# A two-layer attention encoder on one core: the feed-forward in 256x1024 weight tiles, half of them by Strassen's algorithm

## The chip, the core and the metric

The kernel runs on one core of one Trainium2 chip. The core has five engines that work side by side, each with its own queue that it takes strictly in order: TensorE (PE in the profile; its weight loads are shown apart as PEld), VectorE (DVE), ScalarE (ACT), GpSimd (POOL) and SyncE (SP), which here issues most DMAs. Engines wait for each other through semaphores. Matmuls read SBUF and add into PSUM, which has eight banks of 512 float32 columns for each of 128 partitions. The metric is the device time of one execution in microseconds, as a median of several runs; smaller is better. Shares, waits and durations come from a profile of one execution.

## The reference

256 tokens of width 2048 go through two layers, all in float32. Each layer is a norm and an attention, added to x, then a norm and a feed-forward, added to x. The change concerns the feed-forward alone:

```python
D_MODEL = 2048
SEQ = 256
D_FF = 4 * D_MODEL
...
def sq_relu_mlp(h, w1, w2):
    return jnp.square(jax.nn.relu(h @ w1)) @ w2
...
        g, w1, w2 = ffns[i]
        x = x + sq_relu_mlp(rms_norm(x, g), w1, w2)
    return rms_norm(x, final_norm)
```

So per layer there are 256 x 2048 by 2048 x 8192, then 256 x 8192 by 8192 x 2048. Layer 0 has 2-D neighbourhood attention with 16 heads, layer 1 a dilated attention with three groups of eight heads.

## The kernel before

**Two parts for each number.** TensorE multiplies in a format that is rounded against float32 (F32R). Every operand is therefore cut into a rounded part (`hi`, a cast on ScalarE) and the rest (`lo`, a subtraction on VectorE), which is what `split` does (L103 to L105: L104 the cast, L105 the subtraction). A product takes three matmuls: hi by hi, hi by lo, lo by hi.

**Steps.** The program is a list of 400 steps. Each takes one weight block [4 x 128, 512] of 1 MB. `load` fetches it with one DMA on SP's queue into one of three buffers (`wpool`); `prep` cuts one half of it, 1024 columns, into `wh` and `wl`, of which there are four buffers each (`hlpool`). The loop at the end of the program emits, for each step i, its four quarters on TensorE; the first half of step i + 2 is cut behind the second quarter, the other half behind the last, and the load of step i + 5 is issued there too. What else a step carries stands in its lists: `tasks` (a part on TensorE after a quarter, with a part that follows on other engines), `evac` (reads the finished sums), `post`. The order in every engine's queue is the order in which this loop writes it; no scheduler changes it.

**Feed-forward.** It runs over four groups g of 2048 hidden columns, in each of the two layers. A group is 16 steps for w1 and 16 for w2.

- w1 is `gemm_cols`: the weights stand still (each 128x128 piece is loaded into the array), and the activations `xT`, with the 256 tokens' hi and lo side by side, move. Per piece there is a matmul of 512 columns (L134) and one of 256 (L136), 16 such pairs a block. Sums come out with hidden columns on partitions, as the next product needs them. Behind every fourth block two sums each of 512 columns are taken out (a copy on ScalarE at L144, an addition on VectorE at L146), and `done` in `ffn` applies the norm's 1/rms and the squared ReLU (L471, L474) and cuts the result into `hT`.
- w2 is `gemm_rows`: the activations stand still, and the weights move, 24 matmuls of 512 columns a block (`products`, L155 to L157). Sums come out with tokens on partitions and are added to x (L271).

**Norms.** x is transposed on TensorE (L194) and multiplied by the gain, into two parts. 1/rms is applied behind the products. For w1 it is needed along the free axis, so `rows` (L229) spreads it with two small matmuls.

**PSUM.** Three pairs of banks collect sums (`ps_acc`); two single banks (`ps_misc`) serve transposes and attention.

Of the kernel before, what the change touches and what calls it, by code (L numbers as in the profile page):

```python
# [8 lines left out]
F32 = mybir.dt.float32  # L9
# [19 lines left out]
class Step:  # L29
    """One weight block [4 x 128, 512], the products that it takes part in (in four  # L30
    quarters) and the work that goes with them: tasks have a part on the tensor engine
    after a quarter, evac reads the finished sums, post follows."""

    def __init__(self, src, quarters):
        self.src = src
        self.quarters = quarters
        self.evac = []
        self.tasks = [[] for _ in range(4)]
        self.post = []


@with_exitstack
def tile_encoder(ctx: ExitStack, tc: tile.TileContext, ins, out):
    nc = tc.nc

    const = ctx.enter_context(tc.tile_pool(name="const", bufs=1))
    wpool = ctx.enter_context(tc.tile_pool(name="wpool", bufs=3))
    hlpool = ctx.enter_context(tc.tile_pool(name="hlpool", bufs=4))
    big = ctx.enter_context(tc.tile_pool(name="big", bufs=9))
    mid = ctx.enter_context(tc.tile_pool(name="mid", bufs=9))  # L50
    tmp = ctx.enter_context(tc.tile_pool(name="tmp", bufs=2))
    small = ctx.enter_context(tc.tile_pool(name="small", bufs=4))
    ps_acc = ctx.enter_context(tc.tile_pool(name="ps_acc", bufs=3, space=bass.MemoryType.PSUM))
    ps_misc = ctx.enter_context(tc.tile_pool(name="ps_misc", bufs=2, space=bass.MemoryType.PSUM))
# [11 lines left out]
    rope_c = const.tile([32, T], F32, name="rope_c")  # L66
    rope_s = const.tile([32, T], F32, name="rope_s")
# [4 lines left out]
    steps = []  # L72

    def load(i):
        if i >= len(steps):
            return
        s = steps[i]
        s.w = wpool.tile([P, 4, 512], F32, name="w", tag="w")
        s.hi, s.lo = [None] * 2, [None] * 2
        if i:  # L80
            nc.sync.dma_start(s.w, s.src)

    def load_half(i, u):
        nc.sync.dma_start(steps[i].w[:, 2 * u:2 * u + 2, :], steps[i].src[:, 2 * u:2 * u + 2, :])

    def prep(i, u):
        if i >= len(steps):
            return
        s = steps[i]
        hi = hlpool.tile([P, 2, 512], F32R, name="wh", tag="wh")  # L90
        lo = hlpool.tile([P, 2, 512], F32R, name="wl", tag="wl")
        part = s.w[:, 2 * u:2 * u + 2, :]
        if i:
            split(hi, lo, part)
        else:
            for a in range(2):
                split(hi[:, a], lo[:, a], part[:, a])
        s.hi[u], s.lo[u] = hi, lo
# [8 lines left out]
    def three(o, left, right, start, stop):  # L107
        """o += left.T @ right, both in two parts; the product of the two rests is below float32."""
# [5 lines left out]
    def gemm_cols(w, col, xT, nk, done):  # L114
        acc = {}
        made = []
        for k in range(nk):
            def quarter(s, n, k=k):
                if k == 0:
                    if s is steps[0]:  # L120
                        n = (0, 2, 1, 3)[n]
                    if n % 2 == 0:
                        acc[n // 2] = ps_acc.tile([P, 2, 512], F32, name="acc", tag="acc")
# [3 lines left out]
                for j in js:  # L127
                    o = acc[j // 2][:, j % 2, :]
                    cs = slice(j * P, (j + 1) * P)
                    for a in parts:  # L130
# [3 lines left out]
                        nc.tensor.matmul(o, s.hi[a // 2][:, a % 2, cs], xt.rearrange("p h t -> p (h t)"),  # L134
                                         start=first, stop=False)
                        nc.tensor.matmul(o[:, :T], s.lo[a // 2][:, a % 2, cs], xt[:, 0, :],  # L136
                                         start=False, stop=last)
            s = Step(block(w, k, col), quarter)
            steps.append(s)
            made.append(s)  # L140
        for j in range(2):
            def ev(j=j):
                b = tmp.tile([P, 2, T], F32, name="b", tag="b", bufs=2)
                nc.scalar.copy(b, acc[j][:, :, T:])  # L144
                z = tmp.tile([P, 2, T], F32, name="z", tag="z", bufs=2)
# [6 lines left out]
    def products(o, s, xt, a, ts_, start, stop):  # L152
        xh, xl = xt[:, a, 0, ts_], xt[:, a, 1, ts_]
        wh, wl = s.hi[a // 2][:, a % 2, :], s.lo[a // 2][:, a % 2, :]
        nc.tensor.matmul(o, xh, wh, start=start, stop=False)  # L155
        nc.tensor.matmul(o, xh, wl, start=False, stop=False)  # L156
# [674 lines left out]
```

## Time and profile before

| | us |
|---|---|
| median of 3 runs | 2322.12 (2321.59 to 2323.97) |
| span of the profiled execution | 2320.3 |
| busy: PE | 2300.7 |
| busy: DVE | 1406.0 |
| busy: ACT | 1092.6 |
| busy: POOL | 0.7 |
| all PE rows of w1 and of attention, L134 and L136 | 1178.5 and 935.0, x3328 each |
| all PE rows of w2, L155, L156, L157 | 399.5, 399.0, 398.9, x1024 each |

Of the feed-forward, L134 and L136 hold 128 of their 208 blocks. The lengths of matmuls overlap in the trace, since the next begins before the last has drained, so a matmul's price is the distance of starts and not the mean length. The idle time ahead of an engine's instruction is listed with what ended it; on an engine that is not the bound, it costs nothing by itself.

### The profile page before, as it was taken

The numbers are of one execution on the slowest core, as the hardware profiler recorded it, in microseconds if no ns is written. First come the engines' busy times: TensorE is split into PE (matmuls) and PEld (weight loads), VectorE is DVE, ScalarE is ACT, GpSimd is POOL, SyncE is SP. The second block draws the span as 40 slices with busy tenths as digits, with TensorE's granted clock in tenths as the row PEclk, the third lists the DMA queues.
The fourth block names the chain that finished last, engine by engine and source line by source line (L and its number), as shares of the span: only waits on it lengthen the run. The fifth ranks groups of instructions, "written<-read, shape, count | busy, mean of one in ns | idle before, by whom it ended". The sixth has DMA issues, their size and how long they took to land.

```text
span 2320.3 us, 29178 instructions
## 1 busy us (share of the span) xinstructions
PE 2300.7 (99%) x11956; PEld 1963.1 (85%) x11956; DVE 1406.0 (61%) x1635; ACT 1092.6 (47%) x1390; POOL 0.7 (0%) x6
## 2 busy tenths in 40 slices
PE   8999999999999999999999999999999999999998
PEld 7888888888888888888888888888888888888886
DVE  6666765654555555566777667756654654555654
ACT  6444545543443453455444544445543543543443
POOL 0000000000000000000000000000000000000000
PEclk9999999999999999999999999999999999999999
DMA  7555655555555555555555545454555555555553
GB/s 248 169 175 176 191 182 170 182 197 200 182 187 194 185 196 189 193 181 188 189 179 184 177 164 181 164 181 169 191 192 193 182 200 187 189 187 200 200 192 135
DMA packets 73862, 430.36 MB, mean 185 GB/s; under 512 B 19776, under 2 KB 20352, under 8 KB 22528
## 3 DMA queue, kind: packets, MB, share of 16 engines
q1 hardware_dynamic: 73056, 426.80, 54.3%
q8 instruction: 93, 1.52, 0.3%
q10 hardware_dynamic: 672, 1.70, 0.2%
q14 instruction: 41, 0.34, 0.0%
HBM read 426.38 MB, written 2.10 MB: 185 GB/s over the span
## 4 chain that ended last, share of the span: by engine, by line
PE 98%; DMA 1%; DVE 1%; ACT 0%; issue 0%; SPq 0%; ACTq 0%; DVEq 0%
PE acc L134 33%; PE acc L136 17%; PE acc L156 15%; PE acc L155 15%; PE acc L157 15%; PE misc L194 1%; DMA bias<-in_rpb_dram 0%; PE misc L111 0%; PE misc L110 0%; PE misc L109 0%; DVE wl L105 0%; PE misc L593 0%; PE misc L553 0%; PE misc L380 0%; ACT wh L104 0%
## 5 line engine op out<-in xcount | busy, mean ns | idle before, releaser
L105 DVE TENSOR_TENSOR wl<-w,wh 128x1024 fp32r<-128x1024 f32 (+1 forms) x802 | 972.8, 1221 | 735.8 <-ACT wh L104 733.6
L104 ACT CAST wh<-w 128x1024 fp32r<-128x1024 f32 (+1 forms) x802 | 834.9, 1049 | 936.9 <-PE acc L157 460.2
L134 PE MATMUL acc<-xT,wh 128*128 128x512 f32 x3328 | 1178.5, 399 | 0.9 <-ACT wh L104 0.9
L136 PE MATMUL acc<-xT,wl 128*128 128x256 f32 x3328 | 935.0, 281 | 2.3 <-DVE wl L105 2.3
L134 PEld LDWEIGHTS acc<-xT,wh 128*128 128x128 f32 x3328 | 626.4, 188 | 150.4 <-ACT wh L104 1.9
L136 PEld LDWEIGHTS acc<-xT,wl 128*128 128x128 f32 x3328 | 629.8, 189 | 3.7 <-DVE wl L105 3.2
L155 PE MATMUL acc<-wh,hT 128*128 128x512 f32 x1024 | 399.5, 390 | 0.0
L156 PE MATMUL acc<-wl,hT 128*128 128x512 f32 x1024 | 399.0, 390 | 0.0
L157 PE MATMUL acc<-wh,hT 128*128 128x512 f32 x1024 | 398.9, 390 | 0.0
L157 PEld LDWEIGHTS acc<-wh,hT 128*128 128x128 f32 x1024 | 192.3, 188 | 39.9
L155 PEld LDWEIGHTS acc<-wh,hT 128*128 128x128 f32 x1024 | 192.3, 188 | 39.7
L156 PEld LDWEIGHTS acc<-wl,hT 128*128 128x128 f32 x1024 | 192.3, 188 | 39.4
L155 PE MATMUL acc<-wh,xT 128*128 128x512 f32 x320 | 126.7, 396 | 0.0
L156 PE MATMUL acc<-wl,xT 128*128 128x512 f32 x320 | 125.2, 391 | 1.1 <-DVE wl L105 1.1
L157 PE MATMUL acc<-wh,xT 128*128 128x512 f32 x320 | 124.9, 390 | 0.0
L144 ACT COPY b<-acc 128x512 f32<-128x512 f32 x104 | 60.7, 586 | 64.8 <-PE acc L136 59.1
L146 DVE TENSOR_TENSOR z<-acc,b 128x512 f32<-128x512 f32 x104 | 71.5, 691 | 25.8 <-ACT b L144 25.2
L155 PE MATMUL acc<-wh,oT 128*128 128x512 f32 x192 | 76.6, 399 | 0.0
L157 PE MATMUL acc<-wh,oT 128*128 128x512 f32 x192 | 75.0, 391 | 0.0
L156 PE MATMUL acc<-wl,oT 128*128 128x512 f32 x192 | 74.9, 390 | 0.0
L156 PEld LDWEIGHTS acc<-wl,xT 128*128 128x128 f32 x320 | 60.2, 188 | 13.1 <-DVE wl L105 1.8
L157 PEld LDWEIGHTS acc<-wh,xT 128*128 128x128 f32 x320 | 60.1, 188 | 12.5
(123 smaller groups left out, 1044.9 us busy)
## 6 DMA issues: line engine op xcount, KB each, us to landing
w<-in_ffn_w_dram SPq DMA_DIRECT2D x256, 1024.0 KB, 4.8
w<-in_dil_wqkv_dram SPq DMA_DIRECT2D x72, 1024.0 KB, 4.8
w<-in_na_wqkv_dram SPq DMA_DIRECT2D x47, 1024.0 KB, 4.9
w<-in_na_wo_dram SPq DMA_DIRECT2D x16, 1024.0 KB, 4.9
w<-in_dil_wo_dram SPq DMA_DIRECT2D x8, 1024.0 KB, 4.8
bias<-in_rpb_dram SPq DMA_DIRECT2D x32, 96.0 KB, 8.7
out_dram<-x SPq DMA_DIRECT2D x8, 256.0 KB, 2.5
x<-in_x_dram SPq DMA_DIRECT2D x3, 512.0 KB, 7.8
```

Of the source, the lines that this page charges most:

```text
L104: nc.scalar.copy(dst_hi, src)
L105: nc.vector.tensor_tensor(out=dst_lo, in0=src, in1=dst_hi.bitcast(F32), op=ALU.subtract)
L134: nc.tensor.matmul(o, s.hi[a // 2][:, a % 2, cs], xt.rearrange("p h t -> p (h t)"), start=first, stop=False)
L136: nc.tensor.matmul(o[:, :T], s.lo[a // 2][:, a % 2, cs], xt[:, 0, :], start=False, stop=last)
L144: nc.scalar.copy(b, acc[j][:, :, T:])
L146: nc.vector.tensor_tensor(out=z, in0=acc[j][:, :, :T], in1=b, op=ALU.add)
L155: nc.tensor.matmul(o, xh, wh, start=start, stop=False)
L156: nc.tensor.matmul(o, xh, wl, start=False, stop=False)
L157: nc.tensor.matmul(o, xl, wh, start=False, stop=stop)
L194: nc.tensor.transpose(self.tp[:, a, tb * P:(tb + 1) * P], x[:, tb, kt * P:(kt + 1) * P], ident)
```

## The change

**Tiles and forms.** The feed-forward's w1 and w2 both go through a new `gemm_pair`, with activations standing still and tokens on partitions. A step's 1 MB is now a tile of 256 rows by 1024 columns of the weights, loaded by two DMAs of 512 KB. Eight steps make a pair of column blocks (`cp`): four "x" steps, then four "s" steps.

```diff
+    FF_ORDER = [("x", k) for k in range(4)] + [("s", k) for k in range(4, 8)]
+    FF_PAIRS = [k for kind, k in FF_ORDER if kind == "x"]
```

An "s" step is the plain product of 2 x 2 blocks (tokens halves by k halves, k halves by column blocks): 8 products of 3 matmuls, all of 512 columns. An "x" step does the same by Strassen's algorithm in Winograd's form, 7 products of 3 matmuls. It needs sums of weight blocks and of activation blocks. In `X`, each entry is bank, left operand, index of the right:

```diff
+        X = (("1", "A11", 2), ("2", "A12", 3), ("6", "S2", 6), ("7", "S3", 4), ("5", "S1", 5), ("4", "A22", 0),
+             ("3", "S4", 1))
...
+                def quarter(s, m, pair=pair, n=n):
+                    for bank, a, b in X[2 * m:2 * m + 2]:
+                        product(bank, left(pair, a), (s.hi[b], s.lo[b]), n == first_x[-1] and
+                                (bank in "1567" or not first_s))
```

**Cutting the weights.** `prep` now has four parts per step, behind the quarters of the step two ahead of it. An x step makes four sums on VectorE, their rounded parts on ScalarE (`hs`, 1536 columns at once), and rests on VectorE (`ls`) and GpSimd. `sums` has one buffer, `hs` and `ls` have two each. In an s step, GpSimd makes the rests of both halves in even steps and of one half in odd ones; VectorE makes the other:

```diff
+        if n == 0:
+            t = s.sums = part.pool.tile([P, 4, 512], F32, name="sums", tag="sums", bufs=1)
+            add(nc.vector, t[:, 0:2, :], w[:, 1:3, :], w[:, 0, :].unsqueeze(1).to_broadcast([P, 2, 512]))
+            add(nc.vector, t[:, 2, :], t[:, 1, :], w[:, 1, :])
+            add(nc.vector, t[:, 3, :], t[:, 2, :], w[:, 3, :])
+        elif n == 1:
+            hi, lo = two_parts(s, 1)
+            nc.scalar.copy(hi, w[:, 2:4, :])
+            subtract(nc.gpsimd, lo, w[:, 2:4, :], hi.bitcast(F32))
+            s.hs = part.pool.tile([P, 3, 512], F32R, name="hs", tag="hs", bufs=2)
+            nc.scalar.copy(s.hs, s.sums[:, 0:3, :])
+        elif n == 2:
+            ls = part.pool.tile([P, 3, 512], F32R, name="ls", tag="ls", bufs=2)
+            subtract(nc.vector, ls, s.sums[:, 0:3, :], s.hs.bitcast(F32))
...
+            elif s.kind == "s" and (u or s.even):
+                nc.scalar.copy(hi, part)
+                subtract(nc.gpsimd, lo, part, hi.bitcast(F32))
```

**Ends of a pair.** The sums of the x steps (banks 1, 5, 6, 7) are brought together into a tile `C` in SBUF while step s0 runs (`begin`: one copy on ScalarE, four operations on VectorE), and those of all steps (banks 2, 3, 4, S) are added while s3 runs (`end`: four operations on VectorE). A w2 pair then adds C to x with two operations of 1024 columns (`rows`).

**Hidden activations.** Behind a w1 pair, `squared_relu` takes eight operations on ScalarE during the next pair's x0. Then C must be transposed: four groups of four transposes stand in x2 and x3 of the next pair, behind their first and third quarter, all into one PSUM bank. Of the first w1 pair of a group the transposed values are copied out by ScalarE, and `sums_and_parts` makes the sums of activation blocks that the x steps of w2 need; of the second they are only cut in two:

```diff
+                    def post(r=r, held=held):
+                        c, half, pair = 2 * cp + r // 2, r % 2, 4 * cp + r
...
+                        if pair in FF_PAIRS:
+                            raw = scratch([P, 2, T], "h")
+                            nc.scalar.copy(raw, held["t"])
+                            sums[pair] = part.pool.tile([P, 2, 3, P], F32R, name="hs", tag="hsum", bufs=len(FF_PAIRS))
+                            sums_and_parts(raw, hT[c], half, sums[pair], nc.gpsimd)
+                        else:
+                            to = hT[c][:, 2 * half:2 * half + 2]
+                            split(to[:, :, 0, :], to[:, :, 1, :], held["t"])
+
+                    at(i + 2 + r // 2, pe, post, quarter=r % 2 * 2)
...
+        c = scratch([P, 3, P], "c")
+        a11, a21, a12, a22 = raw[:, 0, :P], raw[:, 0, P:], raw[:, 1, :P], raw[:, 1, P:]
+        subtract(nc.vector, c[:, 0, :], a11, a21)
+        subtract(nc.vector, a21, a21, a22)
+        subtract(nc.vector, c[:, 1, :], a11, a21)
+        subtract(nc.vector, c[:, 2, :], a12, c[:, 1, :])
+        hi, lo = (t[:, 2 * half:2 * half + 2, h, :] for h in range(2))
+        nc.scalar.copy(hi, raw)
+        nc.scalar.copy(sums[:, 0], c)
+        subtract(engine, lo, raw, hi.bitcast(F32))
+        subtract(engine, sums[:, 1], c, sums[:, 0].bitcast(F32))
```

**Memory.** PSUM is one tile of eight banks, given out by hand. SBUF has, beside the common tiles, one pool for the attention's tiles and one for the feed-forward's, in the same place, one at a time. 1/rms now applies to partitions, so `rows` (L229) is gone for the norms ahead of the feed-forwards. The attention's arithmetic stays.

**What moves in the queues.** First VectorE's queue where a group's w1 blocks run, before the change. `wl` is a rest of 1024 columns, `z` a sum of 512 that is taken out, `hT` a hidden part; the square brackets name whom an instruction waits for.

```order
L105 TENSOR_TENSOR wl<-w,wh 128x1024 [waits DMAHW7_49,PE_49,Activation_49]
L146 TENSOR_TENSOR z<-acc,b 128x512 [waits Activation_49] x2
L105 TENSOR_TENSOR wl<-w,wh 128x1024 [waits Activation_49]
L471 SCALAR_TENSOR_TENSOR z<-z,rbc 128x512 [waits DVE_49] x2
L105 TENSOR_TENSOR hT<-z,hT 128x2x256 [waits Activation_49] x2
L105 TENSOR_TENSOR wl<-w,wh 128x1024 [waits DMAHW0_49,PE_49,Activation_49]
```

And after the change, VectorE's queue from the rest of a w2 pair's last s step (L192) through the first two x steps of the next pair:

```order
L192 TENSOR_TENSOR wl<-w,wh 128x1024 [waits DMAHW6_49,Activation_49]
L130 TENSOR_TENSOR sums<-w 128x1024 [waits DMAHW1_49,DMAHW0_49]
L130 TENSOR_TENSOR sums<-sums,w 128x512 [waits DVE_49] x2
L127 TENSOR_TENSOR ls<-sums,hs 128x1536 [waits Activation_49]
L127 TENSOR_TENSOR wl<-sums,wh 128x512 [waits PE_49,Activation_49,Pool_49]
L130 TENSOR_TENSOR C<-C,banks 128x512 [waits PE_49]
L130 TENSOR_TENSOR sums<-w 128x1024 [waits DMAHW3_49,DMAHW2_49,DVE_49]
L130 TENSOR_TENSOR sums<-sums,w 128x512 [waits DVE_49] x2
L127 TENSOR_TENSOR C<-banks,C 128x512 [waits PE_49]
L130 TENSOR_TENSOR C<-C,banks 128x512 [waits PE_49]
L127 TENSOR_TENSOR ls<-sums,hs 128x1536 [waits Activation_49]
L130 TENSOR_TENSOR C<-C,banks 128x512 [waits PE_49]
```

Where VectorE had one rest of 1024 per half step, it now has sums, the rest `ls` behind ScalarE's cast of 1536, and the pair's end between them. Right behind these rows come two sums `x<-x,C` of 1024 columns.

Next TensorE's queue before the change, where the last w1 block of a group ends and its first w2 block begins:

```order
L134 MATMUL acc<-xT,wh 128x512
L136 MATMUL acc<-xT,wl 128x256
L134 MATMUL acc<-xT,wh 128x512
L136 MATMUL acc<-xT,wl 128x256
L155 MATMUL acc<-wh,hT 128x512 [waits Activation_49]
L156 MATMUL acc<-wl,hT 128x512 [waits DVE_49]
L157 MATMUL acc<-wh,hT 128x512
```

After the change, TensorE's queue at the third quarter of x2 and the first of x3, in a pair that follows the first w1 pair of a group (`xs` are the sums of activation blocks, `ident<-C` rows the transposes of hidden columns):

```order
L693 MATMUL banks<-ident,C 128x128 [waits Activation_49]
L693 MATMUL banks<-ident,C 128x128 x3
L196 MATMUL banks<-wh,xs 128x512
L197 MATMUL banks<-wl,xs 128x512 [waits Pool_49]
L198 MATMUL banks<-wh,xs 128x512
L196 MATMUL banks<-wh,xT 128x512
L197 MATMUL banks<-wl,xT 128x512 [waits Pool_49]
L198 MATMUL banks<-wh,xT 128x512
```

Before, w2's products followed w1's with nothing between them, and only a block's first products waited, for ScalarE and VectorE. Now the transposes stand between the products, their first one waits for ScalarE, and products of the lower parts wait for GpSimd.

Last ScalarE's queue in the same pair, from the last casts for x3 on. L702 is the copy of a group of transposes, L457 and L458 the rounded parts of hidden values and of their sums, L156 the cast for an s step:

```order
L174 CAST hs<-sums 128x1536 [waits DVE_49,PE_49]
L182 CAST wh<-w 128x512 [waits DMAHW6_49,PE_49,Pool_49]
L183 CAST wh<-sums 128x512 [waits DVE_49]
L702 COPY h<-banks 128x512 [waits PE_49]
L457 CAST hT<-h 128x2x256 [waits DVE_49,Activation_49]
L458 CAST hs<-c 128x384 [waits DVE_49]
L156 CAST wh<-w 128x1024 [waits DMAHW1_49,Pool_49]
L702 COPY h<-banks 128x512 [waits PE_49,Pool_49]
```

The copy that frees the transposes' bank stands behind the cast of VectorE's last sum for x3, and the next copy behind two casts that wait for VectorE and one for an s step. Before the change, ScalarE's queue in w1 blocks held the casts L104, the copies L144 and the squares L474 only.

More of the change, by code (lines that the diff above doesn't have):

```diff
@@ L482, in tile_encoder, with both @@
+            def both(q, tb):
+                return q["C"][:, 2 * tb:2 * tb + 2, :].rearrange("p a n -> p (a n)")
+            for cp in range(2):
+                gemm_pair(w2g, cp, hT, sums, FF_ORDER, lambda made, q, cp=cp: residual(made, q, cp),
+                          split_end=last and next_norm() in fin and cp == 1)
     ffn(norms[1], ins["ffn0_w1"], ins["ffn0_w2"], lambda: norms[2], begin_norm(2, True))
+    parts[len(steps)] = "attention"
     n2 = norms[2]
@@ L703, in tile_encoder @@
             steps[i].tasks[q].append((pe, post))
+    for i, n, f in later_after:
+        steps[i].after[n].append(f)
     def load_x(begin, end):
```

423 lines of the change are left out of this document (297 added, 126 removed).

## The prediction, made before the run

> **What bounds the kernel now.** I read the page first, then the waits, then the stretches of the feed-forward.
>
> ```profile
> span 2320.3 us, 29178 instructions
> PE 2300.7 (99%) x11956; PEld 1963.1 (85%) x11956; DVE 1406.0 (61%) x1635; ACT 1092.6 (47%) x1390; POOL 0.7 (0%) x6
> PEclk9999999999999999999999999999999999999999
> PE 98%; DMA 1%; DVE 1%; ACT 0%; issue 0%; SPq 0%; ACTq 0%; DVEq 0%
> ```
>
> TensorE is busy for 99% of the span at the full granted clock, and 98% of the chain that ended last is its own work. The waits of TensorE that the trace puts down to the engines that cut the weights are tiny, while VectorE spends its idle time waiting for the cast on ScalarE, and ScalarE for TensorE to give a buffer back:
>
> ```profile
> PE acc L136 <- DVE wl L105: 2.3, 3, 0.8
> PE acc L156 <- DVE wl L105: 1.1, 2, 0.6
> DVE wl L105 <- ACT wh L104: 733.6, 606, 3.3
> ACT wh L104 <- PE acc L157: 460.2, 292, 2.2
> ```
>
> So the time before is the number of matmuls times their spacing. What one group g of a feed-forward takes is seen in the stretches of one w1 half and one w2 half (length, then the busy time of PE, PEld, DVE, ACT, POOL, then clock, DMA share and GB/s):
>
> ```profile
> 407.00:495.60 88.60, 88.60 (x516) 77.64 (x515) 53.74 (x65) 47.17 (x60) 0.00 (x0) 1.00 0.54 185
> 495.60:583.00 87.40, 87.40 (x390) 72.48 (x389) 46.76 (x45) 36.86 (x38) 0.00 (x0) 1.00 0.57 193
> ```
>
> That is 88.6 + 87.4, about 176 us, and eight such groups make up some 1406 of the 2320 us. VectorE has about 100 us of work in 176, GpSimd none. The attention layers keep their arithmetic, and I count no change there.
>
> **What TensorE saves.** The spacings are read from starts far apart in steady stretches, since a matmul's own length overlaps the next:
>
> ```profile
> 451.79 0.40 PE L134 MATMUL acc<-xT,wh 128*128 128x512 f32 x1
> 461.49 0.40 PE L134 MATMUL acc<-xT,wh 128*128 128x512 f32 x1
> 699.67 0.39 PE L157 MATMUL acc<-wh,hT 128*128 128x512 f32 x1
> 732.99 0.39 PE L157 MATMUL acc<-wh,hT 128*128 128x512 f32 x1
> 1054.00 0.39 PE L157 MATMUL acc<-wh,hT 128*128 128x512 f32 x1
> 1054.23 0.60 PE L194 MATMUL misc<-ident,x 128*128 128x128 f32 x4
> 1054.59 0.47 PE L155 MATMUL acc<-wh,hT 128*128 128x512 f32 x1
> 1054.90 0.39 PE L156 MATMUL acc<-wl,hT 128*128 128x512 f32 x1
> ```
>
> The first pair of rows spans 28 pairs of L134 and L136: 9.70/28 = 0.346 us a pair, so a w1 block (16 pairs) takes 5.54 us. The second spans 147 matmuls of 512 columns: 33.32/147 = 0.2267 us, so a w2 block (24) takes 5.44 us. After the change every block is in the second form. A standard step keeps 24 matmuls (5.44 us), a Strassen step has 21 (4.76 us). Hidden activations now come out with tokens on partitions, so 64 groups of four transposes are added. A group between such matmuls is seen in the last four rows: 0.90 us from 1054.00 to 1054.90, where two spacings alone are 0.45, so 0.45 us.
>
> Before: 128 x 5.54 + 128 x 5.44 = 1405.8 us. After: 128 x 4.76 + 128 x 5.44 + 64 x 0.45 = 1334.2 us. That saves 71.6 us; the row-broadcast products of norms 1 and 3 go too (two groups, 0.9 us by the same price). If TensorE never waits, each group takes 166.7 us instead of 175.7. **All turns on whether waits of some 9 us per group eat this up.**
>
> **What the other engines must now do.** Prices (name, form, count, busy us, mean ns, then idle time ahead):
>
> ```profile
> L105 DVE TENSOR_TENSOR wl<-w,wh 128x1024 fp32r<-128x1024 f32 x798 | 970.2, 1223 | 735.8 <-ACT wh L104 733.6
> L146 DVE TENSOR_TENSOR z<-acc,b 128x512 f32<-128x512 f32 x104 | 71.5, 691 | 25.8 <-ACT b L144 25.2
> L338 DVE TENSOR_TENSOR bias<-bias,namask 128x1536 f32<-128x1536 f32 x4 | 7.0, 1758 | 23.4 <-DMA bias<-in_rpb_dram 15.8 <-DMA w<-in_na_wqkv_dram 7.6
> L104 ACT CAST wh<-w 128x1024 fp32r<-128x1024 f32 x798 | 832.6, 1051 | 936.9 <-PE acc L157 460.2 <-PE acc L134 452.4 <-issue 9.2
> L104 ACT CAST hT<-z 128x512 fp32r<-128x512 f32 x64 | 36.0, 610 | 0.0
> L474 ACT ACTIVATE z<-z 128x512 f32<-128x512 f32 x64 | 39.5, 633 | 60.6 <-DVE z L471 60.6
> 1217.30 0.68 DVE L519 TENSOR_TENSOR sh<-sh,rb 32x512 f32<-32x512 f32 x1
> 1217.91 0.67 DVE L520 TENSOR_TENSOR qk<-z,ra 128x512 f32<-128x512 f32 x1
> 1218.62 0.68 DVE L521 TENSOR_TENSOR qk<-qk,sh 32x512 f32<-32x512 f32 x1
> ```
>
> In VectorE's queue the next instruction starts 0.61 us behind one of 512 (1217.30 to 1217.91), or 0.71 us behind it when it reads its result (to 1218.62). So 512 elements take 0.61 or 0.71, and with the same 0.07 off, 1024 take 1.15 and 1536 take 1.69. For the cast of 1536 on ScalarE there is no row: from 512 to 1024 elements it grows from 0.61 to 1.05, so 1.49 us is my estimate; its bounds are the 1.05 of 1024 and the 2.1 of two such.
>
> One Strassen step costs VectorE three sums (1.15 + 0.71 + 0.71 = 2.57). The rest ls of 1536 follows, which needs the cast hs, and hs needs the second sum: 1.15 + 0.71 + 0.1 + 1.49 = 3.45 us from the start, so VectorE idles 0.9 us; then ls (1.69) and one 512 rest (0.61). That is 5.75 us of queue time for a step that TensorE does in 4.76. The standard steps cost VectorE 1.15 in every other step, so it catches up there, as far as its buffers let it: ScalarE's cast for step s3 waits for TensorE to finish s1, so VectorE can't begin the next pair's x0 before TensorE is some 2.2 us into s2 (cast 1.05, rest 1.15).
>
> Put t = 0 at TensorE's start of s2 of one pair. TensorE would do s3 from 5.4, x0 from 10.9, x1 from 15.6, x2 from 20.4, x3 from 25.2, and needs ls 1.6 us into a Strassen step (seven matmuls). VectorE: x0 from 2.2 to 8.0; x1 with the four sums of the pair's end (4 x 0.61, of which 0.9 fills the idle time), and behind a w2 pair two sums of 1024 into x (2.3): to 17.6. Its x2 has ls at 17.6 + 5.15 = 22.75, needed at 22.0: wait 0.8. Its x3 begins at 23.35, ls at 28.5, needed at 27.6 with that wait: 0.9. **So a pair behind a w2 pair waits some 1.7 us; two per group, 3.4 us.**
>
> Behind a w1 pair there are no sums into x, but ScalarE has eight instructions of squared ReLU (8 x 0.63 = 5.0 us) in x0, ahead of the casts of x2, so VectorE's x2 ends late as well, at about 22.8, and x3 runs from there: sums to 25.4, hs to 26.2, ls to 28.0. Now the transposes. All four groups use one PSUM bank, so each waits until the one before has been copied out. The copy (ScalarE, first w1 pair) stands in the queue behind the last cast of x3, which ends at 27.2; it ends at 27.7. The second group's turn is at 20.4 + 0.45 + 18 x 0.2267 = 24.9. **Wait 2.8 us.** In the pair behind the second w1 pair the bank is read by VectorE behind x3's last rest (28.6), and free at 29.2: **wait 4.3 us.** Matmuls of x2 and x3 that are ready stand behind these transposes in TensorE's queue.
>
> Behind the first w1 pair comes a chain for each next group: copy 0.6, four sums of 128 columns on VectorE, casts 0.6 and 0.5, rests on GpSimd, in two temporary buffers; the third and fourth copies wait for the rests, and so do the third and fourth transposes and the bank in s0.
>
> GpSimd has no such row, only these:
>
> ```profile
> masks.py:199 POOL TENSOR_SCALAR_AFFINE_SELECT ident<-ident 128x128 f32<-128x128 f32 x1 | 0.3, 292 | 0.1
> masks.py:197 POOL MEMSET ident<- 128x128 f32 x1 | 0.2, 204 | 0.3 <-POOLq L821 0.3
> L821 POOL MEMSET const-float32-1.0<- 128x1 f32 x1 | 0.1, 98 | 0.0
> ```
>
> Against 98 ns for one element, 128 cost 194 ns more in the select, 1.5 ns an element, and 106 more in the memset, 0.8. So 1024 elements take from 0.95 us (memset) over 1.66 (select, one input) to 3.2 (a second input as dear as the first); I take the middle of the last two, 2.4 us. The Trainium skill, GPSIMD Engine Reference, section 3.1, gives 4497 ns for 2048 fp32 elements of a two-input operation, against 2293 ns on VectorE. Halved, that is an estimate of 2.25 us, by which the sum would move by less than 8 us; no run here shows it.
>
> With 2.4 us, the 512 and 384 rests take 1.2 and 0.9, and the chain sets the rhythm: I get further waits of about 1.4, 1.5 and 0.9 us, less if GpSimd is quicker, some 1.5 in all at 1.66 us. I take 2.5. The sum per group is 3.4 + 2.8 + 4.3 + 2.5 = 13.0 us, and x8 it is **104 us given back against 72.5 saved**: 2322.1 - 72.5 + 104 = 2354 us. That stands on the median; the profiled span is 2320.3, 1.8 us less, so the span should read about 2352.
>
> Smaller things I take at nothing: the weights come as two DMAs of 512 KB per step on SP's queue,
>
> ```profile
> w<-in_ffn_w_dram SPq DMA_DIRECT2D x256, 1024.0 KB, 4.8
> ```
>
> and 4.8 us for 1024 KB just fits a Strassen step of 4.76, with three buffers to spread it and longer steps to follow; if that cover goes, at most 0.1 us per Strassen step, 13 us. The phase pools' changeovers could wait once for each of three switches, a few us in all.
>
> **Rivals.** (a) *VectorE keeps ahead.* The place is the 0.9 us that VectorE idles for hs. If the cast of 1536 took 1.05 (its lower bound) or ScalarE began it sooner, VectorE's loop would be 5.2 us or less, x3's last rest would be done some 2 us sooner in pairs behind w2, and the copies some 3 us sooner behind w1. Left would be about 1.3 us for the second w1 pair and 2.5 to 3.3 for the chain behind the first, say 4.5 per group: 2249.6 + 36 = 2286 us. It decides at 9 us per group, that is, where VectorE's loop falls to about 5.3 us. For it: VectorE's load per pair (16 instructions of x steps and the ends, 30 us of 41) leaves room on average, and my waits are differences of large times in which 5% is 1 us. Against it: each price is a row, and every hand-over between engines in the sum costs no less than I put down.
>
> (b) *GpSimd and VectorE get in each other's way.* Before, GpSimd is idle, so nothing in the trace speaks for or against it. VectorE's work with two operands from SBUF is, per group, 16 x 5.05 (x steps) + 8 x 1.22 + 4 x 1.22 + 16 x 0.29 (an estimate for 128 columns) = 100 us; GpSimd's, at 48 x 2.4 + 8.4, is 124 us. If they could only run in turn, 224 us would not fit into 175.7: 48 us per group more, 2322 + 8 x 48 = 2710 us. Half of that would be 2520. It decides from some 76 us of GpSimd's work on, since 100 + 76 makes the 176 of before. The Trainium skill, SBUF — State Buffer, section "Who interferes with whom", states this: a VectorE instruction with two SBUF inputs contends with a GpSimd instruction that reads SBUF, and the later one is blocked for the whole of the other. By that rule the time would be the 2710; no run here shows it yet.
>
> (c) *The two cancel.* Waits between 8.5 and 9.6 us per group leave the time within 0.2% of before, about what a measurement of this kernel can tell from no change.
>
> **How the numbers follow.** The forecast, with waits of 9.6 to 19 us per group (2327 to 2400 us), has a chance of 0.38. (a), below 2317.5, has 0.32: my queue times are good to a few per cent only, and the break-even lies 4 us per group away. (c) has 0.07. (b) has 0.23: 0.11 for partial contention, 2400 to 2560, and 0.12 for more. The bounds of the cast and of GpSimd's price lie within these. To leave out no more than 2 in 10, the range goes from 2266 (below it some 0.07 of (a): 2 us of waits per group) to 2560. The likeliest case's own range is 2327 to 2400. Faster 0.32, same 0.07, slower 0.61.
>
> **What would show it.** In the profile after, TensorE should have about 10,400 instructions and 2230 us of plain work. The waits of TensorE should list the hidden transposes behind ScalarE's copy and VectorE's hT, about 2.8 and 4.3 us at the longest, and ls of Strassen steps at about 0.9. VectorE's wait for hs should be near 0.9 us a step. If (a) holds, those rows shrink to tenths. If (b) holds, means of VectorE's sums and rests rise above the 1223 and 1758 ns of before while GpSimd is busy. I am wrong in the first term if a Strassen step without waits takes other than 4.76 us, and in the sum if the waits stand at loads of weights or at GpSimd's rests of standard steps, which I gave nothing.

## The result, and the profile after

The changed kernel takes 2847.9 us (median of 4, 2846.5 to 2850.47), the kernel before 2322.18. The ratio is **1.2265, interval 1.2247 to 1.2282**: 526 us slower, outside the range that I gave. In the page of the profile after, the lines that answer to the first ones of before:

```profile
span 2848.7 us, 29392 instructions
PE 2413.8 (85%) x10796; PEld 1937.4 (68%) x10796; DVE 2063.6 (72%) x2050; ACT 1338.8 (47%) x1758; POOL 1190.0 (42%) x518
PEclk9999999899899889888999999999999899899998
PE 44%; DVE 27%; issue 12%; ACT 8%; POOL 7%; DMA 1%; POOLq 0%; ACTq 0%; DVEq 0%; SPq 0%
DVE sums L130 13%; PE banks L221 10%; PE banks L197 9%; PE banks L196 9%; PE banks L198 9%; POOL wl L127 6%; PE banks L223 5%; DVE wl L127 5%; ACT hs L174 3%; DVE ls L127 2%; DVE C L130 2%; DVE c L127 2%; DVE wl L192 1%; ACT wh L191 1%; DVE x L130 1%
```

TensorE has 1160 fewer instructions, yet it is busy longer, and it idles for 435 us instead of 20. The chain that ended last now runs through VectorE's sums and GpSimd's rests. The granted clock, 1.0 all through before, falls below 0.9 in ten of the 40 slices. The two feed-forwards, by stretches (length, then the busy time of PE, PEld, DVE, ACT, POOL, then clock, DMA share and GB/s):

```profile
412.40:1383.30 970.90, 768.58 (x3034) 593.48 (x3033) 714.09 (x602) 446.37 (x552) 585.74 (x254) 0.90 0.46 139
1870.80:2838.80 968.00, 764.32 (x3018) 588.83 (x3016) 726.77 (x601) 443.09 (x550) 595.31 (x255) 0.91 0.45 137
```

Each takes about 970 us where, by the same view, the two took 712.6 and 709.8 before; everything outside them adds up to 909.8 us (span less both) against 897.9. So a group takes 242 us, and in it VectorE is busy for 180 and GpSimd for 148. In the groups of the profile by form (form, count, busy us and mean ns, idle time ahead), VectorE's instructions show where the time is:

```profile
L127 POOL TENSOR_TENSOR wl<-w,wh 128x1024 fp32r<-128x1024 f32 x320 | 847.7, 2660 | 1106.2 <-ACT wh L171 1021.8 <-ACT wh L156 76.9 <-DVE rstd L474 6.8
L127 POOL TENSOR_TENSOR hT<-h,hT 128x512 fp32r<-128x512 f32 x32 | 41.1, 1286 | 45.1 <-ACT hT L457 45.1
L130 DVE TENSOR_TENSOR sums<-w 128x1024 f32<-128x1024 f32 x128 | 250.7, 1959 | 2.4 <-DMA w<-in_ffn_w_dram 0.2
L130 DVE TENSOR_TENSOR sums<-sums,w 128x512 f32<-128x512 f32 x256 | 285.3, 1115 | 8.8
L127 DVE TENSOR_TENSOR wl<-sums,wh 128x512 fp32r<-128x512 f32 x128 | 212.3, 1658 | 31.0 <-ACT wh L183 31.0
L130 DVE TENSOR_TENSOR C<-C,banks 128x512 f32<-128x512 f32 x125 | 84.6, 677 | 0.0
```

A sum of 1024 takes 1.96 us in place of 1.22, one of 512 takes 1.12 in place of 0.69, the 512 rest 1.66 in place of 0.69. But `C<-C,banks`, which has one operand in PSUM, takes 0.677 us, no more than the 0.69 of such an instruction before (`z<-acc,b`). The timeline of VectorE, GpSimd and ScalarE in one x step shows how it comes about (start, length, engine):

```profile
1036.54 2.59 POOL L127 TENSOR_TENSOR wl<-w,wh 128x1024 fp32r<-128x1024 f32 x1 [0.17 <-ACT wh L171]
1036.95 3.26 DVE L130 TENSOR_TENSOR sums<-w 128x1024 f32<-128x1024 f32 x1
1040.24 1.42 DVE L130 TENSOR_TENSOR sums<-sums,w 128x512 f32<-128x512 f32 x2
1041.03 1.47 ACT L174 CAST hs<-sums 128x1536 fp32r<-128x1536 f32 x1 [4.56 <-DVE sums L130]
```

GpSimd's rest runs from 1036.54 to 1039.13. VectorE's sum is shown from 1036.95 to 1040.21, which is 1.08 us after GpSimd's end, about its own length: it stood still until GpSimd was done. The next two sums, with GpSimd idle, take 0.7 each, and ScalarE's cast had to wait 4.56 us. The whole trace says the same. 48 of the 128 sums of 1024 began while a rest of GpSimd ran; they are shown with 3.19 us on average and nine in ten of them end 1.079 to 1.086 us behind GpSimd's end. The other 80 take 1.22 us. So the mean of 1.96 mixes sums that were held with sums that were not. 72 of `C<-C,banks` also began beside a running rest, and the longest took 0.683 us. What TensorE waited for, longest first (total, times, longest):

```profile
PE banks L196 <- DVE C L130: 109.7, 59, 3.1
PE banks L693 <- ACT h L702: 74.1, 24, 6.4
PE banks L693 <- DVE hT L192: 71.2, 8, 8.9
PE banks L197 <- DVE ls L127: 36.5, 31, 1.3
```

The hidden transposes (L693) are there, as forecast, but with 3.1 us on average behind ScalarE (24 times) and 8.9 behind VectorE, where 2.8 and 4.3 were worked out; ahead of them stands a wait that I had not counted, for the last sums of a pair to leave PSUM (C).

### The profile page after: what moved, and what is told of

Read it like the earlier page. It is cut to its first block, busy times and chain, and to the rows that moved or that the text cites. A ratio compares the mean times of both kernels' runs of the same rounds, so it can differ in the third digit from the quotient of the medians.

```text
span 2848.7 us, 29392 instructions
## 1 busy us (share of the span) xinstructions
PE 2413.8 (85%) x10796; PEld 1937.4 (68%) x10796; DVE 2063.6 (72%) x2050; ACT 1338.8 (47%) x1758; POOL 1190.0 (42%) x518
## 4 chain that ended last, share of the span: by engine, by line
PE 44%; DVE 27%; issue 12%; ACT 8%; POOL 7%; DMA 1%; POOLq 0%; ACTq 0%; DVEq 0%; SPq 0%
DVE sums L130 13%; PE banks L221 10%; PE banks L197 9%; PE banks L196 9%; PE banks L198 9%; POOL wl L127 6%; PE banks L223 5%; DVE wl L127 5%; ACT hs L174 3%; DVE ls L127 2%; DVE C L130 2%; DVE c L127 2%; DVE wl L192 1%; ACT wh L191 1%; DVE x L130 1%
## 5 line engine op out<-in xcount | busy, mean ns | idle before, releaser
L127 POOL TENSOR_TENSOR wl<-w,wh 128x1024 fp32r<-128x1024 f32 x448 | 1118.6, 2512 | 1593.8 <-ACT wh L171 1021.8
L192 DVE TENSOR_TENSOR wl<-w,wh 128x1024 fp32r<-128x1024 f32 (+1 forms) x354 | 455.3, 1296 | 436.7 <-ACT wh L191 434.9
L191 ACT CAST wh<-w 128x1024 fp32r<-128x1024 f32 (+1 forms) x354 | 366.8, 1045 | 360.3 <-PE banks L198 172.6
L196 PE MATMUL banks<-wh,xT 128*128 128x512 f32 x1024 | 416.3, 407 | 48.9 <-DVE C L130 23.9
L221 PE MATMUL banks<-xT,wh 128*128 128x512 f32 x1280 | 454.5, 398 | 0.8 <-ACT wh L191 0.7
L197 PE MATMUL banks<-wl,xT 128*128 128x512 f32 x1024 | 413.4, 404 | 20.7 <-DVE wl L192 12.1
L198 PE MATMUL banks<-wh,xT 128*128 128x512 f32 x1024 | 409.2, 400 | 0.0
L223 PE MATMUL banks<-xT,wl 128*128 128x256 f32 x1280 | 358.4, 280 | 2.3 <-DVE wl L192 2.3
L196 PE MATMUL banks<-wh,hT 128*128 128x512 f32 x704 | 287.6, 409 | 44.8 <-DVE C L130 37.9
L197 PE MATMUL banks<-wl,hT 128*128 128x512 f32 x704 | 286.2, 406 | 11.1 <-DVE wl L127 7.2
L127 DVE TENSOR_TENSOR ls<-sums,hs 128x1536 fp32r<-128x1536 f32 x128 | 247.6, 1934 | 63.0 <-ACT hs L174 63.0
L198 PE MATMUL banks<-wh,hT 128*128 128x512 f32 x704 | 282.3, 401 | 0.0
L196 PEld LDWEIGHTS banks<-wh,xT 128*128 128x128 f32 x1024 | 199.9, 195 | 105.3 <-DVE C L130 29.8
L156 ACT CAST wh<-w 128x1024 fp32r<-128x1024 f32 x192 | 197.2, 1048 | 125.5 <-PE banks L198 97.8
L127 DVE TENSOR_TENSOR wl<-sums,wh 128x512 fp32r<-128x512 f32 x128 | 212.3, 1658 | 31.0 <-ACT wh L183 31.0
L198 PEld LDWEIGHTS banks<-wh,xT 128*128 128x128 f32 x1024 | 198.9, 194 | 42.4
```

The lines of the kernel that those rows point to most:

```text
L127: engine.tensor_tensor(out=out, in0=a, in1=b, op=ALU.subtract)
L156: nc.scalar.copy(hi, part)
L191: nc.scalar.copy(dst_hi, src)
L192: nc.vector.tensor_tensor(out=dst_lo, in0=src, in1=dst_hi.bitcast(F32), op=ALU.subtract)
L196: nc.tensor.matmul(o, left[0], right[0], start=start, stop=False)
L197: nc.tensor.matmul(o, left[0], right[1], start=False, stop=False)
```

## The experiments

In all of them the time is split in the same way. Before, TensorE is busy 2300.7 us and idle 19.6. From that come the saving that was worked out (72.5 us, or 0.68 per x step where w1 isn't changed), the busy time above what is then left (slower matmuls and slow restarts behind waits), and the idle time above 19.6. These add up to the span.

| run | saving | slower matmuls | more idle | span |
|---|---|---|---|---|
| after | 72.5 | 185.6 | 415.3 | 2848.7 |
| rests_on_vector | 72.5 | 88.7 | 206.4 | 2542.9 |
| gpsimd_only_writes | 72.5 | 50.0 | 130.0 | 2427.8 |
| w2_only_x4 | 43.5 | 39.1 | 78.5 | 2394.4 |
| w2_only_x4_spread | 43.5 | 28.2 | 61.3 | 2366.3 |
| w2_only_x3 | 32.6 | 28.1 | 57.4 | 2373.2 |
| w2_only_x2 | 21.8 | 22.1 | 57.1 | 2377.7 |
| w2_only_x4_early_ends | 43.5 | 29.2 | 51.2 | 2357.2 |
| w2_only_x3_early_ends | 32.6 | 21.6 | 30.9 | 2340.2 |
| w2_only_x3_norm_as_before | 28.6 | 13.3 | 12.8 | 2317.8 |

**Is it the two engines together?** First all rests to VectorE, so that GpSimd is idle:

```diff
-                subtract(nc.gpsimd, lo, part, hi.bitcast(F32))
+                subtract(nc.vector, lo, part, hi.bitcast(F32))
...
-            subtract(nc.gpsimd, lo, w[:, 2:4, :], hi.bitcast(F32))
+            subtract(nc.vector, lo, w[:, 2:4, :], hi.bitcast(F32))
...
-                            sums_and_parts(raw, hT[c], half, sums[pair], nc.gpsimd)
+                            sums_and_parts(raw, hT[c], half, sums[pair], nc.vector)
```

> Edit: every rest that GpSimd makes is made by VectorE. Theory E (exclusion: a VectorE instruction with two SBUF operands and a GpSimd instruction that reads SBUF don't run at once): VectorE's means fall back to 1.22 us (1024 columns), 0.69 (512) and 1.76 (1536); VectorE then has some 180 to 195 us a group, so 2410 to 2500 us. Theory Q (the queues of VectorE and ScalarE are late by themselves, contention counts for little): VectorE gets some 64 us more per group and the time rises above 2850, to 3100 at most. Theory C (a good part is TensorE's clock behind waits): granted clock nearer to 1 than 0.935 only if the waits shrink.

Measured: 2546.19 us, ratio 1.0963 (1.0931 to 1.0995). That is 302 us less than after the change, although VectorE now does GpSimd's work as well. The by-form row of this run:

```profile
L130 DVE TENSOR_TENSOR sums<-sums,w 128x512 f32<-128x512 f32 x256 | 177.2, 692 | 8.7
```

The mean of a 512 sum is that of before again, and VectorE is busy for 2065.1 us, as long as after the change (2063.6), with 512 instructions more. What GpSimd took over had cost VectorE the same time in standing still. The gain is time in which VectorE idles: 478 us (span less busy) in place of 785; ScalarE's cast hs, on which VectorE's next rest depends, waits 316 us for sums in all instead of 569. Theory Q falls. The time is 46 us above theory E's range; the table shows that 89 us of it are slower matmuls, which E had not counted.

**Does GpSimd's reading matter, or its work as such?** In the second run GpSimd fills the same tiles and reads nothing; the kernel leaves out these rests:

```diff
     def subtract(engine, out, a, b):
+        if engine is nc.gpsimd:
+            for _ in range(2):
+                nc.gpsimd.memset(out.bitcast(F32), 0.0)
+            return
         engine.tensor_tensor(out=out, in0=a, in1=b, op=ALU.subtract)
```

> Leaves out GpSimd's rests: in place of each subtraction GpSimd fills the same tile with zeros, twice, so it is kept busy but reads nothing from SBUF. Theory E, with reads as the condition: VectorE's means at 1.22, 0.69 and 1.76 us while GpSimd is busy, and a time of 2300 to 2400 us, near the sum that was forecast without contention. If writing counts too: VectorE's means stay raised and the time stays above 2700. Theory Q: VectorE's and ScalarE's work is the same as after the change, so the time stays above 2700 with VectorE's means at their old values.

Measured: 2429.14 us, ratio 1.0459 (1.0429 to 1.0489). The by-form rows, and what TensorE waited for (this kernel's line numbers are 4 higher: L697 is the hidden transposes, L388 those of a norm):

```profile
L129 POOL MEMSET wl<- 128x1024 f32 x640 | 611.7, 957 | 1414.6 <-PE banks L201 1396.2
L134 DVE TENSOR_TENSOR sums<-sums,w 128x512 f32<-128x512 f32 x256 | 177.1, 692 | 8.7
```

```profile
PE banks L697 <- DVE hT L196: 37.3, 8, 4.9
PE banks L697 <- ACT h L706: 30.4, 12, 3.2
PE banks L201 <- DVE ls L131: 22.7, 26, 1.3
PE banks L388 <- DVE gx L414: 9.0, 4, 3.9
PE banks L388 <- DVE xT L419: 8.9, 2, 5.1
PE banks L388 <- DVE x L485: 6.5, 5, 2.3
```

GpSimd is busy for 803 us, and VectorE's means are those of before: what GpSimd writes does not hold VectorE up. The means show this by themselves; the time does not, for the fills also differ from the rests in waiting for no cast on ScalarE and in being shorter (two of 1024 take 1.91 us, a rest 2.66). With that reserve this run is also the test of my queue sum without contention. The waits are where it put them and nearly as large: 37.3/8 = 4.7 us behind hT (worked out 4.3), 2.5 behind ScalarE's copy (2.8), 0.87 at ls (0.8 and 0.9), in all 90.4/8 = 11.3 us a group (13.0). The wait for C, the longest after the change, is 0.9 us in all here, so it is VectorE's lateness that makes it. Still it is 29 us above the upper end that I expected, by 50 us of slower matmuls and by the norms' transposes (L388) behind attention (xT, x) and behind layer 0's feed-forward (gx), which I had not priced.

**The price by itself.** The kernel before, with GpSimd work beside it that nobody waits for (the attention's temporary buffers go from 5 to 4 to make room for its tile):

```diff
+        if i < 130:
+            nc.gpsimd.tensor_tensor(out=gs, in0=gs, in1=gs, op=ALU.subtract)
+        elif i < 260:
+            nc.gpsimd.tensor_copy(gs, gs)
+        else:
+            nc.gpsimd.memset(gs, 0.0)
```

> The kernel before, with GpSimd work on a tile of its own that nobody waits for, back to back: 260 subtractions of 512 columns (two operands from SBUF), then 260 copies of 512 columns (one operand), then 280 fills (none). Theory E: VectorE's rest of 1024 columns is 1.22 us long beside the fills and behind them, and 1.7 to 2.5 us long in the stretches of the subtractions and of the copies; the time grows by 0 to 1%, since VectorE has room. Theory Q: 1.22 us in every stretch, and 2322 us.

Measured: 2355.25 us, ratio 1.0141 (1.0111 to 1.017). GpSimd's subtractions run until 418 us, its copies until 691, its fills until 855. VectorE's rests of 1024 in four windows, 30 to 440, 440 to 710, 715 to 870 and from 870 us on (at the end of the first, GpSimd has already made 23 of its copies):

```profile
L114 DVE TENSOR_TENSOR wl<-w,wh 128x1024 fp32r<-128x1024 f32 x123 | 208.2, 1714 | 31.9 <-ACT wh L113 31.6
L114 DVE TENSOR_TENSOR wl<-w,wh 128x1024 fp32r<-128x1024 f32 x97 | 139.8, 1457 | 72.6 <-ACT wh L113 72.5
L114 DVE TENSOR_TENSOR wl<-w,wh 128x1024 fp32r<-128x1024 f32 x56 | 68.3, 1225 | 63.2 <-ACT wh L113 63.2
L114 DVE TENSOR_TENSOR wl<-w,wh 128x1024 fp32r<-128x1024 f32 x503 | 611.3, 1223 | 477.5 <-ACT wh L113 477.3
```

1.71 us beside instructions that read two operands, 1.46 beside those that read one, 1.22 beside fills and alone. The order is as theory E says; the copies cost less than expected (1.46 where 1.7 was the lower end). That is no weaker hold: of the 106 rests that began beside a running subtraction, nine in ten end 1.078 to 1.082 us behind its end, and of the 94 beside a copy half end within 1.073 us of its end. But a copy is over sooner (0.62 us unheld, a subtraction 1.04), so less of it is left to wait for. And the time grew by 1.4% where 1% was the upper end, since even with spare time VectorE was late for TensorE now and then.

**Why are matmuls slower?** The kernel before, with waits of growing length made by extra copies on ScalarE, of a small tile of their own that gets its room in the same way:

```diff
+        if u == 0 and i % 12 == 0 and i > 84:
+            for _ in range(4 + i // 12 % 8 * 3):
+                nc.scalar.copy(gs, gs)
```

> The kernel before, with 4 to 25 copies of 512 columns (0.53 us each) put into ScalarE's queue ahead of a cast in every 12th step from step 96 on, so that TensorE waits between 0 and some 8 us there. Theory C: behind waits of some microseconds the granted clock falls to one half for 3 us or more and matmuls start 0.43 us apart, so that the span grows by clearly more than TensorE's idle time. Without C: the clock stays at 1.0 and the span grows by the idle time alone, 40 to 120 us.

Measured: 2407.99 us, ratio 1.0368 (1.0338 to 1.0398). By the page TensorE idles 54.9 us more and is busy 29.2 us more than before, with the same matmuls. TensorE's timeline around one wait, and the stretches before and behind it (the clock is the third value from the end):

```profile
1584.36 0.39 PE L163 MATMUL acc<-wh,xT 128*128 128x512 f32 x1
1589.25 0.79 PE L161 MATMUL acc<-wh,oT 128*128 128x512 f32 x1 [4.50 <-ACT wh L110]
...
1591.53 0.63 PE L161 MATMUL acc<-wh,oT 128*128 128x512 f32 x1
1591.95 0.63 PE L162 MATMUL acc<-wl,oT 128*128 128x512 f32 x1
```

```profile
1560.00:1584.00 24.00, 24.00 (x120) 20.12 (x119) 7.77 (x8) 17.83 (x27) 0.00 (x0) 1.00 0.52 185
1589.00:1595.00 6.00, 5.29 (x12) 3.81 (x13) 4.99 (x5) 5.16 (x8) 0.00 (x0) 0.50 0.24 70
```

Behind a wait of 4.5 us the granted clock is 0.5 for some 7 us, and matmuls start 0.43 us apart instead of 0.23. Theory C holds: a wait costs more than its length.

**What is left without GpSimd and without hidden transposes?** Now w1 in the form of before (with the sums of activation blocks made behind the squared ReLU), w2 in pairs, all rests on VectorE, and x steps varied:

```diff
-    FF_ORDER = [("x", k) for k in range(4)] + [("s", k) for k in range(4, 8)]
+    FF_ORDER = [(kind, k) for k, kind in enumerate("xxxxssss")]
...
-            for cp in range(2):
-                gemm_pair(w1, 2 * g + cp, norm.xT, norm.sums, FF_ORDER, lambda made, q, cp=cp: hidden(made, q, cp))
+                gemm_cols(w1, (4 * g + c) * 512, norm.xT, 4, done)
```

> Edit: w1 goes back to the form of before (no hidden transposes), w2 keeps pairs with xxxxssss, and VectorE makes every rest. Without waits TensorE would need 2322 - 64 x 0.68 = 2279 us. Theory V (what counts is VectorE's work in each stretch, once GpSimd is out and the transposes' bank is not waited for): VectorE has some 43 us of work in a w2 pair of 40.8 us, so it falls behind by the end of the x steps; waits of 2 to 4 us a pair with the clock behind them, 2310 to 2350 us. Rival X (x steps wait wherever they stand): as in the run with all rests on VectorE, 12 us and more per pair, 2450 us or more.

> As w2_only_x4, with the order xxsxxsss, so that VectorE has a standard step to catch up in. Theory V: 5 to 30 us less than w2_only_x4, 2290 to 2330 us. Rival X: no difference to w2_only_x4.

> As w2_only_x4, with three x steps a pair, xxsxssss. VectorE has some 39 us in a pair of 41.5. Theory V: hardly any wait, 2290 to 2310 us, faster than before. Rival X: 2400 us or more.

> As w2_only_x4, with two x steps a pair, xxssssss. VectorE has some 34 us in a pair of 42.2. Theory V: 2300 to 2310 us, no waits beside those of before; the saving is 32 x 0.68 = 21.8 us. Rival X: 2360 us or more.

Measured: 2394.8, 2370.68, 2375.22 and 2379.82 us, ratios 1.0313, 1.0208, 1.0227 and 1.0251, each with an interval of about 0.15% to either side. Theory V fails in all four: above its ranges by 45, 41, 65 and 70 us. Spreading four x steps gained 24 us, as it said, which rival X ruled out; X was also too dear for four and three steps, and right for two. Between three and two x steps VectorE's load falls, but the waits for z and C stay as they are, so there its load isn't what is left. In the run with three, TensorE waits mainly for these, and the timeline shows one case:

```profile
PE banks L196 <- DVE z L233: 29.1, 8, 3.8
PE banks L196 <- DVE C L130: 13.5, 7, 2.9
```

```profile
498.56 1.75 DVE L127 TENSOR_TENSOR ls<-sums,hs 128x1536 fp32r<-128x1536 f32 x1
500.23 1.28 DVE L233 TENSOR_TENSOR z<-banks,b 128x512 f32<-128x512 f32 x2
501.56 0.50 PE L196 MATMUL banks<-wh,hT 128*128 128x512 f32 x1 [3.81 <-DVE z L233]
```

The pair wants all eight banks, and the sums that free w1's last banks (z) stand in VectorE's queue behind ls, 1.7 us long, for the next x step. The same goes for C between two pairs. So the order was changed: the last sums ahead of ls, and the banks that are still in use later in an x step.

```diff
-        X = (("1", "A11", 2), ("2", "A12", 3), ("6", "S2", 6), ("7", "S3", 4), ("5", "S1", 5), ("4", "A22", 0),
+        X = (("1", "A11", 2), ("6", "S2", 6), ("7", "S3", 4), ("5", "S1", 5), ("2", "A12", 3), ("4", "A22", 0),
...
             elif i and n < 3:
-                prep(i + 2, n)
+                hold = n == 2 and s.evac and i + 2 < len(steps) and steps[i + 2].kind == "x"
+                if not hold:
+                    prep(i + 2, n)
+            elif i and hold and s.after[3]:
+                prep(i + 2, 2)
...
+        elif hold and not s.after[3]:
+            prep(i + 2, 2)
         prep(i + 2, 3)
```

> As w2_only_x3, with two orders changed: the last sums of a pair or a w1 block leave PSUM ahead of the rest ls of 1536 columns on VectorE (behind it before), and an x step uses the banks in the order 1, 6, 7, 5, 2, 4, 3. Theory B (what is left in the w2_only runs is bank hand-over: 3.6 us behind each w1 half and 1.8 us behind each first w2 pair, 5.4 us a group, and the clock behind them): these waits fall below 1 us each, some 35 us of waits and 15 to 25 us of clock and restart go, 2305 to 2330 us. If the waits only move to ls or to z: 2355 us or more.

> As w2_only_x4_spread with the same two orders changed. Theory B: 2295 to 2325 us, less than w2_only_x3_early_ends as long as VectorE (43 us of work in 40.8 us of pair) can use the w1 half to catch up. If VectorE is the bound of the pair: 2335 us or more, and more than w2_only_x3_early_ends.

Measured: 2341.2 us (1.0079, 1.0066 to 1.0093) and 2359.48 us (1.016, 1.0146 to 1.0173). With three x steps the run is 34 us faster than before this edit, most of it idle time (57.4 to 30.9 us), as theory B says, though 11 us above its range. With four it gains 11 us only and stays behind three, which is what was expected if VectorE, with 43 us of work in 40.8 by the expectation's estimate, is the bound there. TensorE's waits fit: 23.7 us for VectorE's rests wl (L127) and ls, against 3.8 with three. Last, the hand-over to the next norm as before the change, in the last group of layer 0, and the bank that w1 gives back last used later by the first pair behind w1:

```diff
+            if plain:
+                out_rows(w2g, hT, 4, next_norm, next_done, [(c, k) for c in range(NB) for k in range(4)])
+                continue
...
+        if cp == 0:
+            X = X[:2] + X[6:] + X[2:6]
```

> As w2_only_x3_early_ends, with two edits: the last group's w2 of layer 0, behind which the next norm begins, is computed in column blocks of 512 as before the change (no x steps there, 6 x 0.68 = 4 us given back), and the first pair behind w1 uses the bank that w1 leaves free third. Theory B continued: what was left beside the saving are the waits of the norm between the layers (5.4, 2.4, 3.9 us and shorter, with some 8 us of halved clock) and of VectorE's z (1.1 us a group); these go for the most part, 2312 to 2322 us, equal to before or up to 0.4% faster. If the norm waits in the same way: 2338 us or more.

Measured: 2319.54 us (median of 11; ratio 0.9988, 0.9979 to 0.9997), within the expectation, and the only run ahead of the kernel before, by 0.1%. The norm's waits for gx and x (8.3 and 5.7 us) are gone, those for z fell from 7.6 to 1.8. Its page:

```profile
span 2317.8 us, 29703 instructions
PE 2285.4 (99%) x11830; PEld 1933.3 (83%) x11830; DVE 1671.2 (72%) x2035; ACT 1168.2 (50%) x1509; POOL 0.7 (0%) x6
```

It saves 28.6 us of matmuls by the sum and keeps 2.5, with the clock at 1.0 throughout. Where the rest goes shows in one w2 half, from 674.48 to 760.84 us: 86.4 us for 366 matmuls, which by their spacing need 83.0, where before a half took 87.1 for 384. The idle times shown in it are five of 0.08 to 0.48 us, 1.3 in all. But the start behind each of them comes later than the idle time says, and the one after it is late too. That costs 0.27 to 0.28 us a wait beyond what is shown, and together it is 2.7 of the 3.4 us.

## Why the prediction was wrong

- **What bounds the kernel before, and TensorE's saving**: right in its spacings: away from waits, matmuls of 512 columns start 0.227 us apart in the changed kernels too, which makes 4.76 us for 21. The saving was worked out some 10 us too small. The w1 block of 5.54 us was read in a layer's first group; in the three others 16 blocks take 90.44 us (584.27 to 674.71), 5.65 each. In the first three rows of the table saving and slower matmuls would both be some 10 us larger. TensorE's list has 10,796 instructions where some 10,400 were forecast; the forecast's own terms (7168 matmuls become 5760 and 256 transposes, and 8 go) give 10,796, so that was a slip in counting.
- **The failed step is the use of VectorE's prices of before beside a busy GpSimd.** The sum took 5.75 us of queue time per x step from rows in which GpSimd was idle; contention stood apart as rival (b) with a chance of 0.23, and the range ended at 2560, in the middle of it. The three sums of an x step, 2.57 us in the forecast, are shown with 1.96 + 2 x 1.12 = 4.2 on average (1.22 + 2 x 0.69 = 2.6 unheld). The runs show that it is no matter of degree. In them an instruction of VectorE with two operands from SBUF and one of GpSimd that reads SBUF do not run at once: VectorE's 1024, begun beside such a GpSimd instruction, ends 1.08 us behind its end; the mean is 1.71 us beside subtractions, 1.22 beside fills; the kernel takes 2848 us with GpSimd's rests, 2546 with VectorE making them, 2429 with fills in their place. The Trainium skill, SBUF — State Buffer, section "Who interferes with whom", says that a VectorE instruction with two SBUF inputs contends with a GpSimd instruction that reads SBUF, and not with one that only writes it; the traces agree, also in that instructions with one operand in PSUM keep their 0.68 us.
- **Rival (b)** was the case, and its 2710 us was 138 too low. It added 100 and 124 us of work per group as if the two engines were never both idle. A group took 242 us, and in the two stretches above VectorE and GpSimd stand idle together for 76 and 74 us, 18.7 a group: about what 242 has above 224. Its price of a rest on GpSimd was good: 2.40 us where VectorE doesn't hold it up, as estimated; so was that of the cast of 1536, 1.48 (1.49).
- **The queue waits** (13.0 us a group, 104 in all) were right in place and nearly in size, seen without contention: 2.5, 4.7 and 0.87 us where 2.8, 4.3 and 0.8 to 0.9 stood, 11.3 us a group.
- **Two terms were missing** in the forecast even so. Each wait was counted at its length; it also costs clock and restart, 50 us in gpsimd_only_writes and 186 after the change. And the norms' transposes behind the sublayers wait some 24 us in sum (9.0 + 8.9 + 6.5 above), where I counted no change.
- **Rival (a)**, VectorE ahead, is refuted: even beside fills TensorE idles 130 us more than before. The forecast without contention was 2354; 2429 was measured. That the change came out slower was forecast for a reason that is the smaller part, some 107 of the 526 us; that the forecast had the direction right was in good part luck.

## What to carry to other kernels

Before elementwise work is moved to an idle GpSimd, count VectorE's instructions that take both operands from SBUF: if GpSimd reads SBUF too, add the two engines' times (100 + 124 of a group's 242 us here) instead of laying them side by side. When TensorE is the bound at 99%, a saving in matmuls that adds waits of 2 us and more pays for each of them about one and a half times (415 us of idle time brought 186 us of slower matmuls here), so first give every bank and buffer that it hands over a place in the queue ahead of long work.

## What the runs showed of the hardware

- Waits and the clock. I counted TensorE's waits that had no other wait of over 0.3 us within 9 us ahead or 7 us behind, in all eleven experiments and the run after, and how many were followed within 5 us by a stretch of granted clock 0.5: none of 80 waits of 0.3 to 1.4 us, 3 of 26 from 1.4 to 1.8, 1 of 4 from 1.8 to 2.2, 10 of 13 from 2.2 to 3, 37 of 41 from 3 to 4, and all 25 above. A halved stretch lasted 3.4, 6.8 or 10.2 us. The Trainium skill, TensorE: Matmul & The Clock Gate, section "Why this matters for your kernels", advises against gaps over some 3 us; here the clock also fell behind shorter ones.
- Restart. Behind a wait that the profile shows as 0.83 us, without any fall of the clock, two matmuls start 1.22 us apart and the next 0.34 instead of 0.23, in gpsimd_only_writes:

```profile
573.29 0.39 PE L200 MATMUL banks<-hs 128*128 128x512 f32 x1
574.51 0.50 PE L201 MATMUL banks<-ls,hs 128*128 128x512 f32 x1 [0.83 <-DVE ls L131]
574.85 0.40 PE L202 MATMUL banks<-hs 128*128 128x512 f32 x1
```

  So (1.22 - 0.23) + (0.34 - 0.23) = 1.10 us are lost where 0.83 is shown: this short wait costs 0.27 us more than its row says, as do the five in the w2 half above.
- An instruction that stands still for another engine's reading is shown as busy, not as waiting (3.26 us for a sum of 1.22). VectorE's 72% busy therefore holds standing still as well as work; the mean of a form against the same form elsewhere tells the two apart.
- GpSimd takes 1.29 us for 512 columns with two operands where it isn't held up (row of hT above), and 2.40 for 1024; 1.04 for 512 in gpsimd_beside_before, where one tile is both operands and the output.
